# Gate and up products of both FFNs by a seven-product scheme (Strassen–Winograd), with FFN features in three phases

## The chip, the cores and the metric

The kernel runs on one core of a Trainium2 chip. The metric is the device time of one execution in microseconds; lower is better. The time before is the median of three runs, 1134.87 us (1134.28 to 1135.37). The engines are called as in the profile: PE (matmuls; PEld loads its stationary tiles), DVE and POOL (elementwise), ACT (copies and activations), SP (issues the transfers; it computes nothing).

## What is computed

One decoder block on x of 512 tokens by 1024 features, in f32: a SwiGLU FFN, a token mixer (latent attention beside a short convolution) and a second FFN. Each has a norm that is scaled and shifted by vectors that come from a condition c through `w_ada`, and a gated residual. Cut to what matters here:

```
mod = (silu(c) @ w_ada + b_ada).reshape(b, 3, 3, 1024)          # 72 columns of 128 features
h = rms_norm(x, norm_w[0]) * (1 + mod[:, 0, 1]) + mod[:, 0, 0]
g, u = split(h @ w13[0])                                        # w13: 1024 x 5632
x = x + 0.5 * mod[:, 0, 2] * ((silu(g) * u) @ w2[0])            # w2: 2816 x 1024
x = x + mod[:, 1, 2] * mixer(modulated norm of x)
x = x + 0.5 * mod[:, 2, 2] * swiglu(modulated norm of x, w13[1], w2[1])
```

## The kernel before

**Products.** Features lie on the partitions, tokens on the free axis. The 1024 features of h are 8 chunks of 128; the 2816 features of an FFN are 22 groups of 128, each with a gate and an up part (a pair). Every f32 operand is split into hi + lo, both in a reduced f32 form (fp32r): hi by a copy on ACT (L78), lo by a subtraction on DVE (L79). One 128x128 tile of weights against tokens is then three matmuls, hi·hi, hi·lo and lo·hi (`mm3`, L98 to L101), each over 512 tokens, or over 256 where half of the tokens is taken. Weights come as 512 KB loads (`wr`), and are split one unit of work ahead of their products (`stream`, L314).

**An FFN.** The first pairs (`FIRST`: three in FFN1, two in FFN2) are taken chunk by chunk as the norm delivers h: tiles `pf` of PSUM against weights `wf` that stay in 8 KiB blocks (L412 to L449). FFN1 takes them over 512 tokens at the start of the program, where the norm waits for the first vectors of `mod`; FFN2 takes them in two halves of the tokens, under the second half of the mixer's output and its norm. The other 19 and 20 pairs go through `whole` (L322): the gate over 8 chunks into `p_g`, then the up part into `p_u`, 48 matmuls of 512 columns in a pair; `evac` takes silu of the gate on ACT (`sg`), the product with up on DVE (`av`, L401) and its split into `a`.

**Down products.** `out_rows` (L336) makes the 8 output chunks, `w` in the profile, each over all 22 feature groups, with weights in groups of 8, 8 and 6. The last three chunks of FFN1 and the last one of FFN2 are taken in two halves of 256 tokens, so that the norm of the first half lies under the products of the second. A chunk ends with the residual on DVE (L308) and a store to DRAM.

**Condition vectors.** The shift and scale of the first norm come at the start. The other seven vectors are 56 units of work (`ada_unit`, L206), each 0.5 MB of weights and two multiply-adds of 128x512 on DVE (L159); every eighth ends with transposes on PE and a reduction. FFN1 takes three units with each of its 19 full pairs until all are done (L228), with loads of 1 MB.

**Order.** A scheduler fixes each engine's order from the order of the code and from the pools of buffers: 13 blocks of 8 KiB, 11 and 4 slots of 2 KiB, four loads and four hi and lo tiles of weights, three PSUM banks for long products and five for short ones. Loads are issued by SP in program order as their buffers come free.

The full pairs and the first pairs in the code:

```
units.append(whole(f"g{i}_{f}", (w13a, w13b)[i][f - first, 0], KD, norm.h, gate_done))
units.append(whole(f"u{i}_{f}", (w13a, w13b)[i][f - first, 1], KD, norm.h, up_done))
units += out_rows(f"w2{i}", lambda m: w2[i, m], [(0, 8), (8, 8), (16, 6)], a_pieces, res, next_norm, pace)
...
for t in range(nt):
    mm3(ps[t][:, c0:c1], cols(wf[k], t * P, P), cols(norm.h[k], c0, c1 - c0), k == 0, k == KD - 1)
```

## Time and profile before

| | |
|---|---|
| time, median of three runs | 1134.87 us |
| span of the profiled execution | 1133.9 us |
| last startup chunk split, first full pair of FFN1 | 73.09 us, 78.56 us |
| first down product of FFN1, end of FFN1 | 296.93 us, 421.33 us |
| first full pair of FFN2 | 783.79 us |
| end | 1133.9 us |

The profile is one execution. Its span runs from the first instruction to the last, in microseconds from its start; it lies 1.0 us under the median of the three runs and 0.4 us under the fastest of them (1134.28), so times of the trace and times of runs can be set against each other directly. Groups of instructions are rows "line engine operation out<-in shapes xcount | busy us, mean ns of one | idle time before them". A matmul's end is modelled in this trace, and its row is longer than the time until the next one starts; what a matmul costs in a stream is read from the starts in the timeline.

### The profile page before, as it was taken

Reading aid. Unit: us, or ns where it says so; the run is one execution under the profiler, and the core shown is the slowest. Engines: PE = TensorE matmul, PEld = TensorE weight load, DVE = VectorE, ACT = ScalarE, POOL = GpSimd, SP = SyncE. Lnnn points to the kernel's source line nnn. Section 1 sums busy time; section 2 is a strip of 40 time slices with the busy share of each in tenths; the row PEclk is TensorE's granted clock in tenths of the full one; section 3 lists DMA queues with packets and bytes.
Section 4 is the critical chain, followed back from the end, with each engine's and each line's share of the span. In section 5 each row is a group of like instructions: output and inputs, shape, how many; then the busy total and the mean of one; then the engine's idle time right before and its main releaser. Section 6 shows DMA issues by size and latency. Waiting matters only on the chain.

```text
span 1133.9 us, 14667 instructions
## 1 busy us (share of the span) xinstructions
PE 1106.5 (98%) x5574; PEld 918.5 (81%) x5574; DVE 621.8 (55%) x1143; ACT 410.8 (36%) x774; POOL 68.4 (6%) x76
## 2 busy tenths in 40 slices
PE   4799999999999999999999999999999999999998
PEld 3688788788788998888888778899888888888888
DVE  6976767776533586777556554474333333332233
ACT  4343323333222464544434433353333333322222
POOL 4620000000000003110100000000000000000000
PEclk9889999999999999999999999999999999999999
DMA  8645566655444563221323344671222222224432
GB/s 344 223 149 204 188 241 248 248 189 206 158 137 133 178 204 118 58 83 42 89 98 98 113 139 132 204 231 38 94 93 93 93 93 93 93 84 139 123 119 71
DMA packets 50487, 161.04 MB, mean 142 GB/s; under 512 B 5744, under 2 KB 9712, under 8 KB 45808
## 3 DMA queue, kind: packets, MB, share of 16 engines
q1 hardware_dynamic: 50416, 160.10, 42.1%
q8 instruction: 44, 0.72, 0.3%
q14 instruction: 27, 0.22, 0.1%
HBM read 150.64 MB, written 9.44 MB: 141 GB/s over the span
## 4 chain that ended last, share of the span: by engine, by line
PE 91%; DVE 5%; DMA 2%; issue 1%; ACT 1%; POOL 0%; SPq 0%; DVEq 0%; ACTq 0%
PE w L99 7%; PE w L100 7%; PE w L101 7%; PE p_u L101 6%; PE p_g L99 6%; PE p_g L100 6%; PE p_u L99 6%; PE p_u L100 6%; PE p_g L101 6%; PE p_gate L99 3%; PE p_gate L100 2%; PE p_gate L101 2%; PE pf L99 2%; PE pf L100 1%; PE pf L101 1%; PE p_br L99 1%
## 5 line engine op out<-in xcount | busy, mean ns | idle before, releaser
L79 DVE TENSOR_TENSOR wl_w<-wr_w,wh_w 128x512 fp32r<-128x512 f32 x120 | 77.4, 646 | 142.1 <-ACT wh_w L78 139.3
L99 PE MATMUL w<-a,wh_w 128*128 128x512 f32 (+1 forms) x440 | 153.2, 348 | 0.0
L100 PE MATMUL w<-a,wh_w 128*128 128x512 f32 (+1 forms) x440 | 153.0, 348 | 0.0
L101 PE MATMUL w<-a,wl_w 128*128 128x512 f32 (+1 forms) x440 | 152.9, 348 | 0.0
L78 ACT CAST wh_w<-wr_w 128x512 fp32r<-128x512 f32 x120 | 70.1, 584 | 172.0 <-PE w L100 150.3
L99 PE MATMUL p_g<-hh,wh_g 128*128 128x512 f32 x312 | 123.4, 396 | 0.0
L100 PE MATMUL p_g<-hl,wh_g 128*128 128x512 f32 x312 | 123.4, 396 | 0.0
L101 PE MATMUL p_u<-hh,wl_u 128*128 128x512 f32 x312 | 123.4, 396 | 0.0
L99 PE MATMUL p_u<-hh,wh_u 128*128 128x512 f32 x312 | 123.4, 396 | 0.0
L101 PE MATMUL p_g<-hh,wl_g 128*128 128x512 f32 x312 | 123.4, 396 | 0.0
L100 PE MATMUL p_u<-hl,wh_u 128*128 128x512 f32 x312 | 123.2, 395 | 0.0
L78 ACT CAST wh_u<-wr_u 128x512 fp32r<-128x512 f32 x78 | 48.4, 621 | 143.1 <-PE p_u L100 82.4
L79 DVE TENSOR_TENSOR wl_g<-wr_g,wh_g 128x512 fp32r<-128x512 f32 x78 | 55.1, 707 | 73.8 <-ACT wh_g L78 73.3
L78 ACT CAST wh_g<-wr_g 128x512 fp32r<-128x512 f32 x78 | 48.4, 622 | 129.2 <-PE p_g L100 127.3
L99 PEld LDWEIGHTS w<-a,wh_w 128*128 128x128 f32 x440 | 82.6, 188 | 12.2
L100 PEld LDWEIGHTS w<-a,wh_w 128*128 128x128 f32 x440 | 82.6, 188 | 12.1
L101 PEld LDWEIGHTS w<-a,wl_w 128*128 128x128 f32 x440 | 82.6, 188 | 11.9
L79 DVE TENSOR_TENSOR wl_u<-wr_u,wh_u 128x512 fp32r<-128x512 f32 x78 | 53.4, 689 | 56.2 <-ACT wh_u L78 56.2
L99 PEld LDWEIGHTS p_u<-hh,wh_u 128*128 128x128 f32 x312 | 58.6, 188 | 14.2
L101 PEld LDWEIGHTS p_u<-hh,wl_u 128*128 128x128 f32 x312 | 58.6, 188 | 14.2
L100 PEld LDWEIGHTS p_u<-hl,wh_u 128*128 128x128 f32 x312 | 58.6, 188 | 14.1
L101 PEld LDWEIGHTS p_g<-hh,wl_g 128*128 128x128 f32 x312 | 58.6, 188 | 14.1
(299 smaller groups left out, 2116.0 us busy)
## 6 DMA issues: line engine op xcount, KB each, us to landing
ada<-in_ada_dram SPq DMA_DIRECT2D x36, 1024.0 KB, 8.6
wr_w<-in_w_dram SPq DMA_DIRECT2D x40, 512.0 KB, 3.5
wr_g<-in_w13b_dram SPq DMA_DIRECT2D x20, 512.0 KB, 3.5
wr_u<-in_w13b_dram SPq DMA_DIRECT2D x20, 512.0 KB, 3.5
wr_g<-in_w13a_dram SPq DMA_DIRECT2D x19, 512.0 KB, 3.7
wr_u<-in_w13a_dram SPq DMA_DIRECT2D x19, 512.0 KB, 4.2
wr_gate<-in_w_cg_dram SPq DMA_DIRECT2D x16, 512.0 KB, 3.7
wr_w<-in_w_dram SPq DMA_DIRECT2D x20, 384.0 KB, 3.3
```

Source lines behind the costliest of these rows:

```text
L78: nc.scalar.copy(out=hi, in_=src)
L79: nc.vector.tensor_tensor(out=lo, in0=src, in1=hi.bitcast(F32), op=ALU.subtract)
L99: nc.tensor.matmul(ps, a[0], b[0], start=first, stop=False)
L100: nc.tensor.matmul(ps, a[0], b[1], start=False, stop=False)
L101: nc.tensor.matmul(ps, a[1], b[0], start=False, stop=last)
```

## The change

**Seven products.** A full pair is a 2 by 2 block product: weights in two halves of the contraction (4 chunks each), of gate (G1, G2) and up (U1, U2); h in two halves of the contraction and two halves of the tokens (B11, B12, B21, B22). In place of the eight block products stand seven, each 4 chunks by 3 matmuls of 256 columns, 84 matmuls in a pair (`PRODUCTS`, `pair_job`). They need four sums of weights, Z1 = U1 + U2, Z3 = U1 + G1, Z2 = Z1 + G1 and Z4 = Z2 + G2, and four sums of tokens (t1 to T4). Five 256 KB blocks are loaded plainly by SP (two of them the same block); two DMAs issued by GpSimd then add g1 and u2 onto blocks in SBUF, which gives Z3 and Z1; DVE adds the other two. The splits are three of 128x1024 and one of 128x512 a pair (`split_wide`). The token sums are made once in an FFN (`Norm.sums`: four subtractions or additions of 128x256 on DVE and a split of 128x1024, for each of four chunk pairs). The results are combined on ACT (`s`) and DVE (`y`, `u`, and `g` in its bank).

**Phases.** The features go in three phases (`PHASES`): the pairs of a phase, then its share of all 8 output chunks (`down_job`, all matmuls over 256 columns). The partial sums of the first two phases are stored to DRAM (`yd`), loaded again and added on DVE. Only the last phase has the residual.

**The rest.** `FIRST` is two pairs in both FFNs, and FFN1's are taken in matmuls of 256 columns; `Norm.chunk` makes the shifted x in place, with one more operation on ACT; the weights of FFN2's first pairs have their buffers after the mixer's pool is closed (`enter`), and POOL no longer splits a part of FFN1's. Of the 56 units of condition vectors, 24 stand in the first two down phases of FFN1, in loads of 0.5 MB, and 32 in the mixer's `whole` (`ada_step(1)`).

```
-FIRST = (3, 2)
+FIRST = (2, 2)
+PHASES = (((0, 6), (6, 14), (14, 22)), ((0, 8), (8, 16), (16, 22)))
+PRODUCTS = (("Z3", "T3", 1, 0), ("G1", "B11", 0, 0), ("U2", "T4", 1, 1), ("Z1", "t1", 0, 1),
+            ("Z2", "T2", 1, 0), ("G2", "B21", 0, 0), ("Z4", "B22", 0, 1))
...
+        def sums(self, i):
+            (b11, b12), (b21, b22) = ((x[:, :HALF], x[:, HALF:]) for x in (self.x[i], self.x[i + 4]))
+            t = wide(f"T{self.sub}_{i}")
+            t1, t3, t2, t4 = (t[:, q * HALF : (q + 1) * HALF] for q in range(4))
+            for o, p, q, op in ((t1, b11, b12, ALU.subtract), (t3, b12, b22, ALU.subtract), (t2, t1, b22, ALU.add),
+                                (t4, b21, t2, ALU.subtract)):
+                nc.vector.tensor_tensor(out=o, in0=p, in1=q, op=op)
+            b = block(f"T{self.sub}_{i}", F32R)
+            split_to(b[:, :WMAX], b[:, WMAX:], t)
...
     def whole(name, src, n, rhs, done):
...
                     if k == n - 1:
                         done(ps)
+                        ada_step(1)
...
+        def pair_job(f):
+            def prep(w):
+                sa, sb = block(f"sa{name}"), block(f"sb{name}")
+                g1, g2, u1, u2 = (src[r][:, z * T : (z + 1) * T] for r in range(2) for z in range(2))
+                for s, q, part in ((sa, 0, u1), (sa, 3, u1), (sa, 1, g1), (sa, 2, u2), (sb, 1, g2)):
+                    nc.sync.dma_start(out=s[:, q * T : (q + 1) * T], in_=part)
+                nc.gpsimd.dma_start(out=sa[:, :T], in_=g1, accum_op=ALU.add)
+                nc.gpsimd.dma_start(out=sa[:, 3 * T :], in_=u2, accum_op=ALU.add)
+                a, b = (s.rearrange("p (q n) -> p q n", n=T) for s in (sa, sb))
+                split_wide(w, sa[:, : 2 * T], ("Z3", "G1"), f"w0_{name}")
+                yield
+                nc.vector.tensor_tensor(out=b[:, 0], in0=a[:, 3], in1=a[:, 1], op=ALU.add)
+                split_wide(w, sa[:, 2 * T :], ("U2", "Z1"), f"w1_{name}")
+                yield
+                nc.vector.tensor_tensor(out=b[:, 3], in0=b[:, 0], in1=b[:, 1], op=ALU.add)
+                split_wide(w, sb[:, : 2 * T], ("Z2", "G2"), f"w2_{name}")
+                yield
+                split_wide(w, sb[:, 3 * T :], ("Z4",), f"w3_{name}")
+            def body(w):
+                banks = mm(f"g{name}"), aux(f"u{name}")
...
+                product(0)
+                s = short("sum", 3 * HALF, f"s{name}")
+                nc.scalar.copy(out=s[:, T:], in_=halves[1][0])
+                product(1)
+                yield
+                product(2)
+                product(3)
+                nc.scalar.copy(out=s[:, :T], in_=gate)
+                yield
+                product(4)
...
+                nc.vector.tensor_tensor(out=y, in0=halves[1][0], in1=s[:, :HALF], op=ALU.subtract)
+                nc.vector.tensor_tensor(out=u[:, HALF:].rearrange("p (q n) -> p q n", n=HALF),
+                                        in0=y.unsqueeze(1).to_broadcast([P, 2, HALF]),
+                                        in1=s[:, HALF:].rearrange("p (q n) -> p q n", n=HALF), op=ALU.subtract)
+                nc.vector.tensor_tensor(out=u[:, :HALF], in0=halves[1][1], in1=y, op=ALU.add)
+                product(5)
+                yield
+                product(6)
+                nc.vector.tensor_tensor(out=halves[0][1], in0=halves[0][1], in1=u[:, T:], op=ALU.subtract)
+                evac(f, gate, u[:, :T])
...
+        def down_job(phase, m, c0, c1, n_last):
...
+                for k in range(n):
+                    for h0 in range(c0, c1, HALF):
+                        mm3(ps[:, h0 : h0 + HALF], cols(wt, k * P, P), cols(a_pieces[f0 + k], h0, HALF),
+                            k == 0 and h0 == c0, k == n - 1 and h0 == c1 - HALF)
+                if not final:
+                    y = part[m] if phase else slot(f"y{name}")
+                    if phase:
+                        nc.vector.tensor_tensor(out=y, in0=ps, in1=y, op=ALU.add)
+                    else:
+                        nc.scalar.copy(out=y, in_=ps)
+                    nc.sync.dma_start(out=yd[phase % 2][m], in_=y)
+                    if i == 0:
+                        ada_step(2 if m % 2 == phase % 2 else 1)
```

**Where the instructions move.** First, DVE at the end of FFN1's first pairs. `av_*` and `a_*` are the activations, `wl_g_4` is the lo part of the second full pair's gate weights, `T_*` are the token sums, `sb_2` and `w_0_2_l` the weight sum and lo part of the first full pair (pair 2); each row is the line, the operation, out<-in and the shape. Before:

```order
L401 TENSOR_TENSOR av_0_633<-sg_0_631,pf_1_182 128x512
L401 TENSOR_TENSOR av_1_639<-sg_1_637,pf_3_184 128x512
L79 TENSOR_TENSOR a_0_630<-av_0_633,a_0_630 128x512
L401 TENSOR_TENSOR av_2_646<-sg_2_644,pf_5_186 128x512
L79 TENSOR_TENSOR a_0_630<-av_1_639,a_0_630 128x512
```

And now (where lines are left out before the last two rows, the rope tables stand, L679 to L699):

```order
L338 TENSOR_TENSOR T_3_660<-x_in_74,x_in_75 128x256
L338 TENSOR_TENSOR T_3_660<-T_3_660,x_in_75 128x256
L501 TENSOR_TENSOR av_0_669<-av_0_669,pf_1_182 128x512
L109 TENSOR_TENSOR T_2_657<-T_2_652,T_2_657 128x1024
L338 TENSOR_TENSOR T_3_660<-x_in_75,T_3_660 128x256
L501 TENSOR_TENSOR av_1_674<-av_1_674,pf_3_184 128x512
...
L109 TENSOR_TENSOR T_3_665<-T_3_660,T_3_665 128x1024
L109 TENSOR_TENSOR a_0_668<-av_0_669,a_0_668 128x512
L109 TENSOR_TENSOR a_0_668<-av_1_674,a_0_668 128x512
...
L534 TENSOR_TENSOR sb_2_718<-sa_2_717 128x512
L109 TENSOR_TENSOR w_0_2_l<-sa_2_717,w_0_2_h 128x1024 x2
```

The weights of the first full pair were split ahead of the first pairs' activations; now they are split behind all token sums, activations and rope tables.

Second, SP in FFN1's down products. `wr_w` and `wr_d` are down weights, `ada` and `wr_ada` the condition's weights, `yd` stores of partial sums. Before:

```order
L83 DMA wr_w_0_2_2463<-in_w_dram 128x768
L209 DMA ada_4_2323<-in_ada_dram 128x2048
L209 DMA ada_6_2407<-in_ada_dram 128x2048
L83 DMA wr_w_0_0_2499<-in_w_dram 128x1024
L83 DMA wr_w_0_1_2533<-in_w_dram 128x1024
L83 DMA wr_w_0_2_2568<-in_w_dram 128x768
```

Now, in the first phase:

```order
L113 DMA wr_d_0_5_0_1463<-in_w_dram 128x768
L113 DMA wr_ada_6_1484<-in_ada_dram 128x1024
L625 DMA yd_0_179<-yd_0_4_0_1481 128x512
L113 DMA wr_ada_7_1488<-in_ada_dram 128x1024
L113 DMA wr_d_0_6_0_1532<-in_w_dram 128x768
L625 DMA yd_0_179<-yd_0_5_0_1550 128x512
L113 DMA wr_ada_0_1553<-in_ada_dram 128x1024
L113 DMA wr_d_0_7_0_1583<-in_w_dram 128x768
```

Down weights, condition weights and stores of partial sums now alternate, where the condition weights had nearly all come beside the pairs.

Third, DVE in a full pair of FFN1. Before (pair 7 being prepared, pair 6 being finished):

```order
L159 SCALAR_TENSOR_TENSOR ada_acc_1_961<-ada_0_958,c_act,ada_acc_1_961 128x512
L79 TENSOR_TENSOR wl_g_7_512_1006<-wr_g_7_999,wh_g_7_512_1005 128x512
L79 TENSOR_TENSOR wl_u_7_0_1052<-wr_u_7_1049,wh_u_7_0_1051 128x512
L401 TENSOR_TENSOR av_6_1037<-sg_6_1035,p_u_6_1009 128x512
L79 TENSOR_TENSOR wl_u_7_512_1056<-wr_u_7_1049,wh_u_7_512_1055 128x512
L79 TENSOR_TENSOR a_6_1034<-av_6_1037,a_6_1034 128x512
```

Now (pair 13 being prepared, pairs 11 and 12 being finished):

```order
L109 TENSOR_TENSOR w_0_13_l<-sa_13_2469,w_0_13_h 128x1024
L501 TENSOR_TENSOR av_11_2433<-av_11_2433,u_11_2398 128x512
L534 TENSOR_TENSOR sb_13_2470<-sa_13_2469 128x512
L109 TENSOR_TENSOR a_10_2306<-av_11_2433,a_10_2306 128x512
L564 TENSOR_TENSOR y_12_2525<-u_12_2442,s_12_2455 128x256
L537 TENSOR_TENSOR sb_13_2470<-sb_13_2470 128x512
L565 TENSOR_TENSOR u_12_2524<-y_12_2525,s_12_2455 128x512
L568 TENSOR_TENSOR u_12_2524<-u_12_2442,y_12_2525 128x256
L109 TENSOR_TENSOR w_0_13_l<-sb_13_2470,w_0_13_h 128x1024
L572 TENSOR_TENSOR g_12_2441<-g_12_2441,u_12_2524 128x256
L109 TENSOR_TENSOR w_0_13_hl<-sb_13_2470,w_0_13_hl 128x512
L501 TENSOR_TENSOR av_12_2560<-av_12_2560,u_12_2524 128x512
```

The condition's multiply-adds are gone from the pairs, and the combination of the seven products stands among the splits of the next pair's weights; `y` needs the fifth product of the pair in work, and what stands behind it in the row waits with it.

More of the change, by code (lines that the diff above doesn't have):

```diff
@@ L230, in ada_step, with chunks, __init__, x @@
             ada_unit(*ada_todo.pop(0))
+    def chunks(tiles):
+        return [tiles[k // 4][:, (k % 4) * T : (k % 4 + 1) * T] for k in range(KD)]
     class Norm:
-        def __init__(self, sub, x):
-            self.sub, self.x, self.acc, self.last, self.steps = sub, x, None, {}, iter(())
-            self.h = []
+        def __init__(self, sub, tiles):
+            self.sub, self.acc, self.steps = sub, None, iter(())
+            self.tiles = tiles
+            self.h, self.pairs, self.tsums = [], [], []
+        @property
+        def x(self):
+            return chunks(self.tiles)
         def add(self, k, c0=0, n=T):
@@ L285, in prepare, with operand @@
+        def operand(self, name, i):
+            which, q = OPERANDS[name]
+            b = (self.pairs, self.tsums)[which][i]
+            return tuple(b[:, z * WMAX + q * HALF : z * WMAX + (q + 1) * HALF] for z in range(2))
         def prepare(self, b0, nb):
@@ L455, in ffn @@
             rope_tables()
-        drain(rest)
+        run(jobs)
     rope_tab = {}
@@ L517, in tile_hybrid_block @@
     r1 = Residual(1, xT, 2, x1d)
-    n1 = Norm(1, r1.x)
-    ffn(0, n0, ((0, T),), first_chunk, 3, r1, n1, (0, 1, 1, 2, 2, 2, 1, 0, 0))
+    n1 = Norm(1, r1.tiles)
+    ffn(0, n0, ((0, T),), first_chunk, r1, n1, (0, 2, 3, 3))
+    next(n1.steps)
+    enter("mixer")
     wc = []
@@ L795, in tile_hybrid_block @@
     drain(latent_products(0))
-    next(n1.steps)
     second = latent_products(1)
```

233 lines of the change are left out of this document (166 added, 67 removed).

## The prediction

> **What bounds the kernel now.** I read the page's first part and the chain of waits first, then windows by stage, then the groups by form, then the starts in the timeline.
>
> ```profile
> span 1133.9 us, 14667 instructions
> PE 1106.5 (98%) x5574; PEld 918.5 (81%) x5574; DVE 621.8 (55%) x1143; ACT 410.8 (36%) x774; POOL 68.4 (6%) x76
> PE 91%; DVE 5%; DMA 2%; issue 1%; ACT 1%; POOL 0%; SPq 0%; DVEq 0%; ACTq 0%
> ```
>
> PE is the bound nearly everywhere: 98% busy and 91% of the chain. So matmul time that goes is worth its full price, unless another engine or the DMAs take its place. The windows show who is near to that (columns: PE, PEld, DVE, ACT and POOL busy, granted clock, DMA share, GB/s):
>
> ```profile
> 80.00:200.00 120.00, 120.00 (x528) 96.60 (x527) 84.67 (x154) 38.37 (x66) 2.81 (x8) 1.00 0.59 224
> 380.00:410.00 30.00, 30.00 (x265) 29.95 (x263) 19.38 (x37) 15.85 (x30) 0.84 (x1) 1.00 0.67 200
> 410.00:500.00 90.00, 88.60 (x572) 79.97 (x571) 70.34 (x164) 50.31 (x123) 14.82 (x11) 1.00 0.35 110
> 740.00:775.00 35.00, 34.14 (x283) 33.84 (x282) 28.82 (x62) 18.08 (x36) 2.16 (x2) 1.00 0.62 196
> 900.00:1000.00 100.00, 100.00 (x430) 80.60 (x429) 35.87 (x53) 32.49 (x54) 0.00 (x0) 1.00 0.28 90
> ```
>
> In FFN1's pairs DVE is 71% busy and the DMAs 59%; in FFN2's pairs 36% and 28%. Both have room there, little at the start of the mixer (DVE 78%) and before FFN2 (82%). GB/s over share gives what the DMA engines move at full use: 380 in 80:200, 321 in 900:1000, 299 in 380:410.
>
> The groups give counts; a matmul's end is modelled, so its price is read from starts.
>
> ```profile
> L99 PE MATMUL p_g<-hh,wh_g 128*128 128x512 f32 x312 | 123.4, 396 | 0.0
> L99 PE MATMUL w<-a,wh_w 128*128 128x512 f32 x264 | 104.2, 395 | 0.0
> L99 PE MATMUL w<-a,wh_w 128*128 128x256 f32 x176 | 48.9, 278 | 0.0
> ```
>
> ```profile
> 24.02 2.50 PE L99 MATMUL pf<-hh,wfh 128*128 128x512 f32 x5
> ...
> 29.39 0.51 PE L101 MATMUL pf<-hh,wfl 128*128 128x512 f32 x1
> ...
> 78.56 0.40 PE L99 MATMUL p_g<-hh,wh_g 128*128 128x512 f32 x1
> ...
> 199.61 0.39 PE L99 MATMUL p_u<-hh,wh_u 128*128 128x512 f32 x1
> ...
> 204.28 0.39 PE L101 MATMUL p_u<-hh,wl_u 128*128 128x512 f32 x1
> ...
> 296.93 0.39 PE L99 MATMUL w<-a,wh_w 128*128 128x512 f32 x1
> ...
> 763.82 0.28 PE L101 MATMUL pf<-hh,wfl 128*128 128x256 f32 x1
> ...
> 765.98 0.28 PE L101 MATMUL pf<-hh,wfl 128*128 128x256 f32 x1
> ...
> 783.79 0.40 PE L99 MATMUL p_g<-hh,wh_g 128*128 128x512 f32 x1
> ...
> 1117.76 0.28 PE L100 MATMUL w<-a,wh_w 128*128 128x256 f32 x1
> ...
> 1130.45 0.28 PE L101 MATMUL w<-a,wl_w 128*128 128x256 f32 x1
> ```
>
> From 199.61 to 204.28 are 20 steps, 233.5 ns; over longer stretches I read 233.3. From 1117.76 to 1130.45 are 112 steps of 256 columns, 113.3 ns; from 763.82 to 765.98 are 18, 120.0 ns. So half the columns cost a little under half in one place and a little over half in the other. From 24.02 to 29.39, after PE had idled, 13 steps of 512 columns take 413 ns each: the clock is granted low for a while.
>
> **The change, part by part.**
>
> *Pairs.* Each matmul group of `p_g` and `p_u` has 312: 6 x 312 / 48 = 39 pairs, 39 x 48 x 233.3 ns = 436.8 us. Now 40 pairs of 84 matmuls. The two rows bound their price: 113.3 where the stationary tile lies in the streamed pool (`wh_w`), 120.0 where it lies in a long-lived block (`wfh`). The new weights are streamed tiles, so I take 115: 40 x 84 x 115 = 386.4 us, a gain of 50.4 (17.6 less at 120.2, 5.7 more at 113.3). The seven-for-eight saving needs 84 matmuls of 256 to beat 48 of 512, that is, under 133.3 ns each; both rows are under it.
>
> The Trainium skill, page "TensorE: Matmul & The Clock Gate", section "Back-to-back issue gap", gives sustained streams with weight loads 81 ns at 128 columns and 131 at 512; a straight line between them, an estimate, is 98 ns at 256, and by it a pair would grow from 6.3 to 8.2 us. The trace contradicts it: 512 columns take 233.3 ns here, not 131.
>
> *Down products.* 3 x 264 of 512 and 3 x 176 of 256 columns: 184.8 + 59.8 = 244.6 us. Now 2112 of 256 at 113.3: 239.3, a gain of 5.3 (14.6 less at 120.2).
>
> *FFN1's start.*
>
> ```profile
> 70.03 0.69 DVE L79 TENSOR_TENSOR wl_u<-wr_u,wh_u 128x512 fp32r<-128x512 f32 x1
> 70.63 0.22 DVE L147 TENSOR_TENSOR mod<-ps,pk 128x1 f32<-128x1 f32 x2
> ...
> 73.09 0.75 DVE L283 SCALAR_TENSOR_TENSOR hl<-ht,mod,hh 128x512 fp32r<-128x512 f32 x1 [0.79 <-ACT hh L282]
> ...
> 760.03 0.48 DVE L308 SCALAR_TENSOR_TENSOR x<-wo,mod,xin 128x256 f32<-128x256 f32 x1
> 760.42 0.48 DVE L283 SCALAR_TENSOR_TENSOR hl<-ht,mod,hh 128x256 fp32r<-128x256 f32 x1
> ```
>
> ```profile
> L79 DVE TENSOR_TENSOR wl_w<-wr_w,wh_w 128x512 fp32r<-128x512 f32 x100 | 69.0, 690 | 117.2 <-ACT wh_w L78 114.4 <-PE w L100 2.7
> L159 DVE SCALAR_TENSOR_TENSOR ada_acc<-ada,c_act,ada_acc 128x512 f32<-128x512 f32 x98 | 68.0, 746 | 0.0
> L79 DVE TENSOR_TENSOR wl_w<-wr_w,wh_w 128x256 fp32r<-128x256 f32 x20 | 8.5, 425 | 24.8 <-ACT wh_w L78 24.8
> L79 DVE TENSOR_TENSOR wo<-wr_wo,wo 128x1024 fp32r<-128x1024 f32 x3 | 3.7, 1219 | 0.1
> ```
>
> Back to back, a 512 split takes 0.60 us from start to start (70.03 to 70.63), 0.09 under its 690 ns; so I count 0.34 for 256 columns, 1.13 for 1024, and 0.40 for a 256 step with a scalar (760.03 to 760.42). The last chunk's split ends at 73.84. Now four 512 splits fewer stand ahead of it (-2.4), three token sums more (+1.0), and one ACT step more lies in its chain (+0.7): 73.1. By DVE's order there follow 10 of the sums (3.4), the four 1024 splits of them (4.5), two `av` and two `a` (2.4), the rope tables (20 small steps, 2.2 by the 0.22 us for two at 70.63), a weight sum (0.6) and the first lo part (1.1): 14.2, so the third matmul of the first full pair waits until about 87 (84 to 91; POOL gives up its share of the startup and 1 MB less is loaded, which may bring it forward). In place of 78.56: +8.4. The former cover, a third pair in `pf`, is gone. PE idles some 12 us and then runs at the low clock: +2.3, as the 13 steps of 413 ns lost 0.18 us each.
>
> *FFN2's start.* After the last output chunk is taken at 760.03, DVE now still has: rest of the first half's chunks (2.8), eight 512 splits of `wf` (4.8), the norm and the second half's chunks (6.5), 16 sums and four splits (10.0), `av` and `a` (2.4), a weight sum and the first lo (1.7): 28.2, and some 3 of waits for loads whose buffers come late: 792 in place of 783.79, +8.2 (4 to 13), and +2 at the low clock.
>
> *Pairs on DVE.* By durations a pair asks three 1219, one 690 (splits), two 690 (weight sums), 425 + 690 + 425 + 425 (combination), two 690 (`av`, `a`): 9.1 us; back to back 8.0. A pair on PE takes 9.66, or 9.81 with the stalls below. DVE's work fits by 0.6 to 1.7 us, but in a fixed order: `y` waits for the fifth product, 6.9 us into the pair, and a sum and splits of the next pair stand behind it. Following the rows by hand, every second pair's last lo part comes 0.3 to 0.7 us late: I take +6 over 40 pairs (0 to 12).
>
> *The adding DMAs* have no like in this trace. Bound below: nothing. They wait for plain loads of the same block, and splits wait for them; but blocks are loaded a pair ahead, 9.7 us.
>
> ```profile
> wr_w<-in_w_dram SPq DMA_DIRECT2D x40, 512.0 KB, 3.5
> wr_br<-in_w_br_dram SPq DMA_DIRECT2D x16, 256.0 KB, 2.6
> x1d<-x SPq DMA_DIRECT2D x5, 256.0 KB, 2.1
> ```
>
> A plain load of 256 KB lands in 2.6 us; above: at 3.7 times that the add would use up the pair's lead. I take nothing, nearest to the plain row. The Trainium skill, page "DMA: Bandwidth & Descriptors", section "Anatomy of one DMA — SWDGE (gpsimd) path", gives 2.0 us + bytes / 436e3 for GpSimd's DMAs, 2.6 us for this size as an estimate: by it the term would be nothing too; no run here shows it yet. The pairs' demand, seven blocks of 0.26 MB in 9.7 us, is 190 GB/s, under any rate above.
>
> *FFN1's first two down phases.* PE: 8 x 36 and 8 x 48 matmuls, 32.6 and 43.5 us. DMA in them: down weights 2.8 and 4.2 MB, condition weights 6.3 and 6.3, the next two pairs 3.7 and 3.7, partial sums 2.1 and 4.2: 14.9 and 18.4 MB. At 350 GB/s (between 321 and 380) 42.6 and 52.6 us, 19 more than PE; some 7 us of it is loaded early. I take +12 (2 to 34: at 380 with all pair loads early, at 299 with none). FFN2's phases carry no condition weights: they fit.
>
> *Condition vectors.* FFN1 loses 32 units and four rounds of transposes: of the 5.5 us that 78.56 + 19 x 11.2 leaves until 296.93, 3.1 go to the mixer. There 64 steps of 512 (0.66 each) are 42 us more for DVE, over 340 us where it has room outside 410:500; PE pays the 3.1, I add 2 for DVE and 2 for the exchange of pools: FFN1 -3.1, mixer +7 (3 to 17).
>
> *Sum:* -50.4 - 5.3 - 3.1 + 8.4 + 2.3 + 8.2 + 2 + 6 + 12 + 7 = -12.9, from 1133.9 to 1121.0; runs lie 1.0 above the profiled span: **1122**.
>
> **The rivals.**
>
> *All is covered:* matmuls at 113.3, no pair stalls, no phase stalls: 5.7 + 6 + 12 = 23.7 less, 1098. For: DVE and DMA averages fit. Against: the order of `y`.
>
> *The pair is paced by DVE* (slower side): by durations it has 9.1 of 9.66 us, and each split waits for its ACT copy first. It decides from a pair of 9.81 + 12.9 / 40 = 10.1 us on; at 10.6 it costs 32: 1154. For: six kinds of hand-over between ACT, PE and DVE in a pair, in one fixed order. Against: back to back it is 8.0.
>
> *DMA paces the first two phases* at 299 GB/s, as 380:410 moved with stores among the loads: 34 in place of 12, 1144.
>
> *256 columns cost 120.2*, as in `pf`: 17.5 + 14.6 more, 1154. Against: `w`, the nearest like, is at 113.3.
>
> *A matmul has a high fixed price*, so that half the columns cost three quarters (175 ns by 233.3): 84 x 175 is 3.5 us a pair more than now, +140. The Trainium skill's section on the back-to-back gap, cited above, would have it so. The rows at 113.3 and 120.0 all but exclude it.
>
> *The saving isn't there* because PE is busy by name only: excluded by steady starts at 233.3.
>
> **How the numbers follow.** Forecast 60%, of which 4% lie within 0.2% (2.3 us, about what a measurement can tell from no change); all covered 14%; DVE-paced pairs 10%; DMA-paced phases 8%; 120.2 ns 6%; the last two together 2%. Faster: 56 + 14 = 70%; slower: 10 + 8 + 6 + 2 = 26%. The range, 1098 to 1150, takes in the forecast with its bounds, half of the covered case and the DMA-paced one.
>
> **What would show it.** Pairs: starts 113 to 116 ns apart, 9.7 to 10.1 us a pair; over 10.1 DVE or a DMA ends PE's waits, and the row before the late split says which. FFN1's first full pair at 84 to 91 behind an idle PE that waits for `w_0_2_l`; FFN2's at 788 to 797 less what came earlier. In phases 0 and 1 of FFN1 a DMA share near 1 with PE waiting for `d_0` or `d_1` splits. If PE's idle time sums to much over 50 us, I am wrong on the costs; if its busy time hardly falls, on the gain.

## The result, and the profile after

The changed kernel takes 1225.78 us (median of four runs, 1225.02 to 1230.59); the kernel before took 1135.12 beside it. The ratio is 1.081, 95% interval 1.0795 to 1.0824: slower by 91 us, where 1122 was forecast and at most 1150 was in the range. The profiled execution has a span of 1223.7 us.

The changed kernel's page, its first part, its transfers, and the chain that ended last:

```profile
span 1223.7 us, 20051 instructions
PE 1090.4 (89%) x7886; PEld 1014.9 (83%) x7886; DVE 809.3 (66%) x1393; ACT 497.8 (41%) x835; POOL 133.3 (11%) x149
q1 hardware_dynamic: 79648, 181.61, 45.2%
q0 software_dynamic: 11520, 20.98, 9.9%
PE 61%; DMA 16%; DVE 13%; issue 4%; ACT 3%; POOL 2%; SPq 1%; DVEq 0%; POOLq 0%; ACTq 0%
```

PE has 61% of the chain in place of 91%: DMA has 16% in place of 2%, DVE 13% in place of 5%. No engine is full. So this isn't an engine that became the bound; it is waits. Where they lie shows in the starts of the first and last products of each stage (the row's last bracket is the wait ahead of it):

```profile
84.44 0.28 PE L132 MATMUL pf<-h,wfl 128*128 128x256 f32 x1
...
96.31 0.58 PE L130 MATMUL u<-T,w_h 128*128 128x256 f32 x1 [11.60 <-ACT w_h L108]
...
146.79 0.28 PE L130 MATMUL d<-a,d_h 128*128 128x256 f32 x1
...
206.01 0.28 PE L130 MATMUL u<-T,w_h 128*128 128x256 f32 x1
...
285.97 0.28 PE L130 MATMUL d<-a,d_h 128*128 128x256 f32 x1
...
353.66 0.28 PE L132 MATMUL g<-h,w_l 128*128 128x256 f32 x1
...
436.01 0.28 PE L130 MATMUL d<-a,d_h 128*128 128x256 f32 x1
...
490.76 0.72 PE L130 MATMUL pc<-wc,h 128*128 128x416 f32 x1 [4.10 <-ACT wc L108]
...
861.56 0.58 PE L130 MATMUL pf<-h,wfh 128*128 128x256 f32 x1 [4.91 <-ACT wfh L108]
...
891.04 0.39 PE L130 MATMUL u<-T,w_h 128*128 128x256 f32 x1 [2.65 <-ACT w_h L108]
```

Stage by stage, from these rows and their like in both traces (the mixer runs from the start of FFN1's last product to that of the last `wo` product, 421.2 to 759.3 us before and 483.8 to 856.4 now):

| stage | before | after | difference | forecast, stalls of it included |
|---|---|---|---|---|
| until FFN1's first full pair | 78.6 | 96.3 | +17.8 | +10.7 |
| FFN1's full pairs (19 before, 20 now) | 218.4 | 212.8 | -5.6 | -19 |
| FFN1's down products | 124.3 | 174.7 | +50.4 | +10 |
| mixer | 338.1 | 372.6 | +34.5 | +7 |
| FFN2 until its first full pair | 24.5 | 34.7 | +10.2 | +10.2 |
| FFN2's full pairs | 224.0 | 195.2 | -28.8 | -28 |
| FFN2's down products to the end | 126.1 | 137.5 | +11.4 | -3 |

The saving is there where it was looked for, in FFN2's pairs. The stages that lost add up to 124 us, of which FFN1's down products have 50, the mixer 34, FFN1's start 18, and FFN2's start and down products 10 and 11; the pairs gave back 34. The waits of PE in FFN1's first two down phases, first 146:210 and behind the gap 286:350 (engine, what waits <- for what: us in total, times, longest):

```profile
PE d L130 <- ACT d_h L108: 7.4, 3, 4.5
PE d L130 <- ACT a L108: 2.7, 1, 2.7
PE d L132 <- DVE d_l L109: 2.6, 4, 1.4
...
PE d L132 <- DVE d_l L109: 5.3, 3, 3.7
PE d L130 <- ACT d_h L108: 3.8, 3, 3.0
PE d L130 <- ACT a L108: 3.7, 1, 3.7
```

And those of SP's queue in 146:210:

```profile
SPq L625 <- ACT yd L624: 45.4, 8, 9.5
```

PE waits for the hi and lo parts of down weights (`d_h`, `d_l`). SP stands for 45.4 of 64 us at the stores of partial sums (L625), each of which waits for ACT's copy (`yd`), and so for the end of a chunk's products. What stands behind in SP's row waits too, as some of its starts show:

```profile
155.92 0.33 SPq L625 DMA_DIRECT2D yd<-yd  x1
156.30 0.42 SPq L528 DMA_DIRECT2D sb<-in_w13a_dram  x1
156.82 0.41 SPq L113 DMA_DIRECT2D wr_ada<-in_ada_dram  x1
162.03 0.33 SPq L625 DMA_DIRECT2D yd<-yd  x1
162.45 0.38 SPq L113 DMA_DIRECT2D wr_d<-in_w_dram  x1
166.24 0.33 SPq L625 DMA_DIRECT2D yd<-yd  x1
```

And by stretches (columns as in the prediction): those two phases, and for comparison a stretch of FFN1's pairs:

```profile
147.00:206.00 59.00, 43.94 (x296) 41.47 (x295) 23.91 (x36) 12.01 (x17) 1.73 (x2) 0.86 0.65 203
286.00:354.00 68.00, 52.85 (x400) 50.57 (x398) 31.96 (x45) 9.47 (x11) 1.72 (x2) 0.92 0.74 225
...
220.00:280.00 60.00, 59.70 (x515) 59.30 (x514) 49.17 (x72) 33.41 (x49) 6.93 (x8) 1.00 0.59 149
```

The DMA engines are busy 65% and 74%, not full, and the granted clock (third column from the right) falls to 0.86 and 0.92: behind waits PE runs at half clock for a while. Over the whole execution the low clock was granted for 114 us, 14 before.

### The profile page after: what moved, and what is told of

Read it like the earlier page. It is cut to its first block, busy times and chain, and to the rows that moved or that the text cites. A ratio compares the mean times of both kernels' runs of the same rounds, so it can differ in the third digit from the quotient of the medians.

```text
span 1223.7 us, 20051 instructions
## 1 busy us (share of the span) xinstructions
PE 1090.4 (89%) x7886; PEld 1014.9 (83%) x7886; DVE 809.3 (66%) x1393; ACT 497.8 (41%) x835; POOL 133.3 (11%) x149
## 3 DMA queue, kind: packets, MB, share of 16 engines
q1 hardware_dynamic: 79648, 181.61, 45.2%
## 4 chain that ended last, share of the span: by engine, by line
PE 61%; DMA 16%; DVE 13%; issue 4%; ACT 3%; POOL 2%; SPq 1%; DVEq 0%; POOLq 0%; ACTq 0%
DMA sa<-in_w13a_dram 5%; DMA wr_ada<-in_ada_dram 5%; PE d L132 4%; PE d L131 4%; PE d L130 4%; PE g L132 4%; PE g L130 4%; PE g L131 4%; PE u L132 4%; PE u L131 4%; PE u L130 4%; DMA wr_d<-in_w_dram 2%; DMA sa<-in_w13b_dram 2%; PE p_gate L132 2%; PE p_gate L130 2%
## 5 line engine op out<-in xcount | busy, mean ns | idle before, releaser
L130 PE MATMUL d<-a,d_h 128*128 128x256 f32 x628 | 182.0, 290 | 22.2 <-ACT d_h L108 11.7
L132 PE MATMUL d<-a,d_l 128*128 128x256 f32 x628 | 181.4, 289 | 9.8 <-DVE d_l L109 9.7
L131 PE MATMUL d<-a,d_h 128*128 128x256 f32 x628 | 180.5, 287 | 1.0 <-DVE a L109 0.7
L130 PE MATMUL u<-T,w_h 128*128 128x256 f32 x480 | 134.3, 280 | 14.3 <-ACT w_h L108 14.2
L130 PEld LDWEIGHTS d<-a,d_h 128*128 128x128 f32 x628 | 124.7, 199 | 24.6 <-ACT d_h L108 13.3
L132 PE MATMUL u<-T,w_l 128*128 128x256 f32 x480 | 135.2, 282 | 3.8 <-DVE w_l L109 3.5
L132 PEld LDWEIGHTS d<-a,d_l 128*128 128x128 f32 x628 | 124.4, 198 | 12.0 <-DVE d_l L109 11.9
L131 PE MATMUL u<-T,w_h 128*128 128x256 f32 x480 | 133.9, 279 | 0.0
L131 PEld LDWEIGHTS d<-a,d_h 128*128 128x128 f32 x628 | 124.8, 199 | 2.0 <-DVE a L109 2.0
L109 DVE TENSOR_TENSOR w_l<-sa,w_h 128x1024 fp32r<-128x1024 f32 x80 | 96.7, 1224 | 12.1 <-PE d L131 4.2
L130 PEld LDWEIGHTS u<-T,w_h 128*128 128x128 f32 x480 | 91.3, 190 | 14.9 <-ACT w_h L108 14.7
L132 PEld LDWEIGHTS u<-T,w_l 128*128 128x128 f32 x480 | 91.2, 190 | 6.3 <-DVE w_l L109 6.3
L130 PE MATMUL g<-h,w_h 128*128 128x256 f32 x320 | 90.2, 282 | 6.9 <-ACT s L559 6.5
L131 PEld LDWEIGHTS u<-T,w_h 128*128 128x128 f32 x480 | 91.1, 190 | 0.0
L131 PE MATMUL g<-h,w_h 128*128 128x256 f32 x320 | 89.9, 281 | 0.0
```

Of the source, the lines that this page charges most:

```text
L109: nc.vector.tensor_tensor(out=lo, in0=src, in1=hi.bitcast(F32), op=ALU.subtract)
L130: nc.tensor.matmul(ps, a[0], b[0], start=first, stop=False, skip_group_check=parts)
L131: nc.tensor.matmul(ps, a[0], b[1], start=False, stop=False, skip_group_check=parts)
L132: nc.tensor.matmul(ps, a[1], b[0], start=False, stop=last, skip_group_check=parts)
```

## The experiments

Two theories stood against each other for the phases: Q, that the loads come late because they stand in SP's row behind stores that wait for results, and its rival, that there are too many bytes for the time. For the start, theory O is that the order of POOL's and DVE's work (the rope tables ahead of the first pairs) delays the adding DMAs; for the mixer, theory W is that DVE waits there for the condition weights' loads. Stage lengths below are from the starts of PE's rows, as in the table; the mixer stage is here taken from the first `pc` product to the first `pf` product of FFN2 (370.8 us in the changed kernel). A time without an interval is one run, and a stage length is read from one trace: four runs of the kernel with the orders together lay between 1187.5 and 1199.5, and mixer stages of kernels that leave the mixer alone between 368.6 and 373.5, so differences of this size between single runs say nothing. One fact has to stand ahead of the others: the step of a matmul, the time from its start to the next one's, depends on where its weights lie in SBUF (below, "the address"). The kernels here keep the addresses of the changed kernel, unless said.

**Stores of partial sums on ACT.**

```
-nc.sync.dma_start(out=yd[phase % 2][m], in_=y)
+nc.scalar.dma_start(out=yd[phase % 2][m], in_=y)
```

> The stores of partial sums are issued by ACT in place of SP; nothing else is changed. Theory Q (SP's order: the next chunk's down weights are issued only behind the store of a chunk that PE has yet to finish): FFN1's first two down phases, 59 and 62 us in the changed kernel, come to 36 to 46 and 46 to 53; FFN2's, 45 and 50, to 44 to 46 each; time about 1190. Rival B (bytes: the transfers of the phases take longer than their products): FFN1's phases stay at 55 or more each, time over 1215.

1205.5 us. The two phases took 54.1 and 59.0 us (59.2 and 67.7 in the changed kernel; the 62 of the expectation leaves out the end of the second), FFN2's 44.7 and 49.7. SP's order costs something, about 14 us of these phases, but theory Q foresaw 36 to 46 in the first, and the time lies between the two theories. With the stores gone, SP waits mostly for buffers that PE's products still read:

```profile
SPq L113 <- PE d L132: 16.2, 4, 5.6
SPq L113 <- DMA yd<-yd: 8.1, 4, 4.7
SPq L113 <- PE d L131: 5.2, 1, 5.2
```

**Without condition vectors.** `ada_todo = []`, and constants in `mod` for the seven vectors.

> All 56 units of the condition vectors are left out (their loads, multiply-adds, transposes); the seven vectors are constants. Theory B (bytes): FFN1's first two down phases fall to 33 to 36 and 44 to 46 us. Theory Q (SP's order): the stores still stand ahead of the down weights, which only land sooner: 42 to 54 and 48 to 56. For the mixer, 366 us from its first to its last product against 338 before: if the units there cost it, 338 to 345; if it lost for another reason (the exchange of pools, the split form), 355 or more. Time 1140 to 1165 if the units explain both, over 1190 if neither.

1170.6 us. The mixer fell from 372.6 to 340.8 by the stages of the table, so the units cost it there. But FFN2's pairs, which the edit doesn't touch, had become slower, 205 us in place of 195. The starts in the pairs show why:

```profile
230.00 0.28 PE L132 MATMUL g<-h,w_l 128*128 128x256 f32 x1
230.12 0.28 PE L130 MATMUL g<-h,w_h 128*128 128x256 f32 x1
230.24 0.28 PE L131 MATMUL g<-h,w_h 128*128 128x256 f32 x1
230.36 0.28 PE L132 MATMUL g<-h,w_l 128*128 128x256 f32 x1
```

120 ns everywhere, where the changed kernel has 113 to 118. The edit had also dropped two tiles of 32 bytes that stood ahead of the weight buffers, which so moved by 64 bytes. So its stages don't compare with the changed kernel's. The same kernel, with the addresses kept:

> As the kernel without condition vectors (all 56 units left out, constants in their place), but two small tiles are kept so that the streamed weights lie at the addresses of the changed kernel, 64 bytes off a multiple of 128; in the run before this one they had slid to a multiple of 128, and every matmul of 256 columns there took 120 ns, every one of 512 took 226.5. Theory A (the address of the stationary tile sets the step): 113.3 and 233.3 ns again, about 1142. Rival (the step came from something else in that run): 120 and 226.5 again, about 1170. With 113.3, FFN1's first two down phases at 33 to 38 and 44 to 48 us would lay their loss on the units wholly.

1158.7 us, with 113 to 118 ns in place of 120, and 233 for 512 columns. The address does set the step, but not to the last ns: the median was 117 here and 113 in the changed kernel, FFN2's pairs took 200.6 us, and the time missed 1142; what makes 117 of 113 stays open. FFN1's first two down phases took 35.9 and 49.8 us, the mixer stage 343.7 in place of 370.8. So the 56 units cost 23 + 18 us in the phases and 27 in the mixer, 68 together. Not all of it is the price of their new places: the kernel before has these units too, and pays at least for their transposes (5.5 us by the prediction's reading); it wasn't run without them.

**Loads or multiply-adds.** Two halves of that: the units' loads alone (`raw_load` stays, `scale_add` and the rest go), and their arithmetic alone, on a tile that is on chip.

> The 56 units' loads stay, their multiply-adds, transposes and reductions are left out (constants in place of the vectors), addresses as in the changed kernel. If the loads cost it (bytes, or the buffers and SP's places they take): FFN1's first two down phases stay at 52 or more and 58 or more us. If DVE's waits for these loads cost it (lo parts of the down weights stand behind a multiply-add that waits): 34 to 44 and 45 to 52. The mixer: 340 to 350 if the multiply-adds cost it there, 358 or more if the loads' turns in its four buffers do. Time 1150 to 1165 if DVE, over 1180 if the loads.

> The other half: the 56 units' multiply-adds, transposes and reductions stay but read a tile that is on chip, their loads are left out (the seven vectors are not the reference's). If the loads cost it: FFN1's first two down phases at 33 to 40 and 44 to 50 us, and the mixer at 340 to 350. If DVE's work itself costs it: the phases at 45 or more and 55 or more, the mixer at 358 or more. Time 1145 to 1165 if the loads or the waits for them, over 1190 if the work.

1189.2 and 1166.4 us.

| | first phase | second phase | mixer stage |
|---|---|---|---|
| changed kernel | 59.2 | 67.7 | 370.8 |
| loads only | 52.4 | 70.1 | 344.6 |
| arithmetic only | 34.1 | 52.0 | 355.2 |
| neither | 35.9 | 49.8 | 343.7 |

In the phases it is the loads: by themselves they cost 16.5 of the 23.3 us in the first and all of it in the second, the arithmetic by itself some 2 at most. In the mixer it is the arithmetic (11.5 us by itself, of which 3.3 are the steps of its transposes on PE), and with the loads as well 27; the loads alone cost 1.

**Half the bytes.** `raw_load(ada[v - 2, k // 2][:, k % 2, :T], T, ...)`, each unit using its half twice.

> Each of the 56 units loads half of its columns and uses them twice (so the seven vectors are not the reference's): the same count of loads, multiply-adds and buffers, half the bytes. If bytes cost it in FFN1's first two down phases (59 and 68 us from the first down product to the next pair, 36 and 50 without units): 47 to 50 and 57 to 60. If the places in SP's order and in the ten buffers cost it, whatever their size: 55 to 59 and 63 to 68.

1204.3 us; the phases at 48.5 and 55.6. Halving the bytes gives back 10.7 of 23.3 and 12.1 of 17.9 us, 46% and 68%. So the rival of bytes has the larger part of what the units cost in the phases. Even so the DMA engines weren't full (0.65 to 0.74 busy in the changed kernel). The reading that fits both, which no run shows by itself: loads stand one behind the other, each issued when a buffer or a store lets it, and each holds up the next for as long as its bytes take. The stores' place in SP's row is a part of that chain (14 us).

**Eight plain products in the same structure.** No sums of weights or tokens, no adding DMAs, no combination; all else as changed.

```
+PRODUCTS = (("G1", "B11", 0, 0), ("G1", "B12", 0, 1), ("U1", "B11", 1, 0), ("U1", "B12", 1, 1),
+            ("G2", "B21", 0, 0), ("G2", "B22", 0, 1), ("U2", "B21", 1, 0), ("U2", "B22", 1, 1))
...
+for s, q, part in ((sa, 0, g1), (sa, 1, u1), (sa, 2, g2), (sa, 3, u2)):
+    nc.sync.dma_start(out=s[:, q * T : (q + 1) * T], in_=part)
```

> The changed kernel with eight plain block products of 256 columns in a pair (96 matmuls), no sums of weights or tokens, no adding DMAs, no combination; phases, units, order and buffers as changed. By the starts alone a pair takes 10.9 us in place of 9.5, +54 us over 40 pairs. If the seven products do bring their matmuls' time: pairs of FFN2 11.0 each (9.8 in the changed kernel), and FFN1's first full pair, without sums of tokens, at 84 to 90 in place of 96.3; the phases as before within 5 us; time 1250 to 1275. If the sums and the combination eat it: pairs no more than 0.5 us longer, time under 1235.

1207.7 us: faster than the changed kernel by 18, against both expectations. FFN2's pairs took 10.9 us as the count of matmuls says (87.0 for eight, 77.2 with seven products), so the seven products do bring their time: 25 us in FFN2 and 14 in FFN1's pairs. But FFN1's first full pair started at 84.8 in place of 96.3, its first two down phases took 41.5 and 50.8 in place of 59.2 and 67.7, and FFN2's second 43.5 in place of 50.3. The page has what is gone from the transfers:

```profile
span 1205.9 us, 20054 instructions
PE 1119.2 (93%) x8366; PEld 1050.4 (87%) x8366; DVE 606.3 (50%) x1033; ACT 391.3 (32%) x667; POOL 63.3 (5%) x69
q1 hardware_dynamic: 73888, 171.12, 42.6%
```

No adding DMAs (21.0 MB), and 10.5 MB less in plain loads. So 11.5 + 34.6 us of loss in FFN1, and 10.2 in FFN2's down products, belong to the seven products and no other part of the change. What of the seven products it is, no run takes apart. One part is bytes, seven blocks for a pair in place of four: the two phases of FFN1 moved 9.1 and 13.0 MB here (223 GB/s in 41 us, 255 in 51) where the changed kernel moved 12.0 and 15.3. Another stands in the changed kernel's trace, in DVE's row. Its waits for the adding DMAs of the next phase's pairs, in 146:210 and in 286:350, and two such places with what stood behind them:

```profile
DVE sb L534 <- DMA sa<-in_w13a_dram: 7.7, 2, 4.4
...
DVE sb L534 <- DMA sa<-in_w13a_dram: 14.8, 2, 9.9
```

```profile
308.24 0.69 DVE L534 TENSOR_TENSOR sb<-sa 128x512 f32<-128x512 f32 x1 [9.92 <-DMA sa<-in_w13a_dram]
308.85 0.69 DVE L622 TENSOR_TENSOR yd<-d,yd 128x512 f32<-128x512 f32 x1
309.56 0.33 SPq L625 DMA_DIRECT2D yd<-yd  x1
...
1080.00 0.69 DVE L534 TENSOR_TENSOR sb<-sa 128x512 f32<-128x512 f32 x1 [5.72 <-DMA sa<-in_w13b_dram]
1080.61 0.68 DVE L501 TENSOR_TENSOR av<-av,u 128x512 f32<-128x512 f32 x1
```

The weight sum `sb` of the next phase's pair stands in DVE's fixed order ahead of work that PE and SP need now: the sum of partial results `yd` (SP stood 10.4 us at its store), lo parts of down weights, and the last pair's activation `av`. In FFN2's second phase that makes nearly all of the 6.8 us: PE waits 3.4 us for `a`, with half the clock granted from 1081 to 1088. With eight products these waits of DVE are gone, and its waits for condition weights are not (16.8 us in the first phase of either kernel).

**Rope tables later.** `rope_tables()` behind the third full pair (`if i == 0 and f == 4`) in place of ahead of the first.

> The rope tables are made behind the third full pair of FFN1 in place of ahead of the first; nothing else is changed. Theory O (in-order ACT and POOL: the first pair's hi copy stands behind the rope's sine on ACT, the second pair's adding DMAs stand behind the rope's products on POOL): first full pair at 92 to 94 in place of 96.3, the stall of 6.7 us at 105.9 gone, the low clock behind it shorter; time 10 to 16 less, about 1212. Rival (the second pair's adds are late because its blocks come free late, or because an adding DMA itself is slow): the stall of 6 us stays, time 2 to 4 less.

1211.1 us. The first full pair starts at 91.6; the stage of FFN1's first four pairs 41.7 in place of 50.5, its stall of 6.5 us gone. Theory O holds. In the changed kernel POOL's row shows it:

```profile
95.06 1.04 POOL L708 TENSOR_TENSOR rt_qsin<-pk,rope_tmp 128x64 f32<-128x64 f32 x2 [23.30 <-ACT rope_tmp L701]
...
99.14 2.03 POOL L708 TENSOR_TENSOR rt_kcos<-pk,rope_tmp 128x64 f32<-128x64 f32 x2
101.11 0.87 POOL L529 DMA_DIRECT2D sa<-in_w13a_dram  x1
```

The adding DMAs of the second full pair are instructions of POOL and stood behind six us of rope products (95.06 to 101.11), which stood behind ACT's sine, which stood behind DVE's rope steps.

**The mixer's condition weights in blocks,** in 1 MB loads as in the kernel before, issued by SP, and then by GpSimd:

```
+both = block(f"ada_{v}_{k}")
+nc.sync.dma_start(out=both.rearrange("p (u c) -> p u c", u=2), in_=ada[v - 2, k // 2])
```

> In the mixer the condition weights come as 1 MB loads into 8 KiB blocks, as in the kernel before, in place of the four buffers that the mixer's own weights use; nothing else is changed. Theory W (the loads take turns with the mixer's weights in four buffers, come late, and DVE's multiply-adds stand waiting for them with the attention's steps behind): the mixer, 366 us, comes to 340 to 352, DVE's wait for these loads from some 22 us there to under 6; time about 1205. Rival D (the 64 multiply-adds, 42 us, are simply too much for DVE there): 360 or more, time over 1218.

> In the mixer the condition weights come in 1 MB loads into 8 KiB blocks, issued by GpSimd in place of SP; nothing else is changed. If what stays of the mixer's loss lies in SP's order (its weights' loads behind loads that wait for a block): the mixer, 367 us with the same loads on SP, comes to 352 to 358, time 1208 to 1214. If the transfers' presence beside DVE's work costs it otherwise: 363 or more, time over 1219.

1225.7 and 1220.8 us; the mixer stage 366.6 and 364.5 (370.8). DVE's waits for these loads in the mixer fell from 21.9 us to 4.0 and 5.2, and only 4 to 6 us came back, little more than single traces differ by: theory W falls, and SP's order isn't it either. The arithmetic's 11.5 us stand; why loads beside it add some 10 to 15 more stays open. In the changed kernel PE's waits there are mostly for late steps of the attention (`pTl` 7.0 us and `kTl` 4.6, both from DVE).

**Units back in FFN1's pairs,** three to each, none elsewhere.

> One part of the change undone: the condition vectors' units stand three to a full pair of FFN1, as in the kernel before, and in none of its down phases nor in the mixer. FFN1's first two down phases come to about 36 and 50 us and the mixer to about 344, as without units: 69 us less. DVE then has 8.0 to 9.1 us and 3 x 1.3 in each of 19 pairs, 12 to 13.1 us, so FFN1's pairs, 213 us together, come to 245 to 265. Time 1188 to 1208. If DVE's waits for these loads add to its work, the pairs take over 270 and the time is over 1212.

1281.9 us. The phases fell to 42 and 54 and the mixer stage to 343, but the pairs took 319 us: 15.9 each, more than DVE's work asks. In 203:329 DVE is busy 70% and PE 75%:

```profile
203.00:329.00 126.00, 93.88 (x699) 89.27 (x697) 87.68 (x135) 42.33 (x60) 12.20 (x14) 0.85 0.64 196
```

The units share ten 4 KiB buffers with the pairs' hi and lo parts, and loads of pairs stand behind units in SP's row; from 96 to 330 us DVE stood 37.9 us at the same sum `sb`, whose block came late. None of the places tried is free for the units in this layout; FFN2's first pairs, for the vector that is needed last, weren't tried.

**Orders together.** First three: stores on ACT, rope late, and the start's condition loads ahead of the first pairs' weights; then the first two alone; then these two with the mixer's blocks by GpSimd.

> The changed kernel with three changes of order and none of work: stores of partial sums issued by ACT, rope tables behind the third full pair, and at the start each chunk's condition load issued ahead of the first pairs' weights. If the gains of the first two add up (20.3 and 14.6 against 1225.8) and the third brings FFN1's first full pair forward by 2 to 5 us: 1185 to 1190. Rival (the stalls take each other's place): over 1195.

> Stores of partial sums on ACT and rope tables behind the third full pair, without the third change of order, which put FFN1's first full pair back from 91.6 to 96.3. If the two add up: 1189 to 1193, first full pair at 91.6. Rival: near 1200, as with three.

> The orders that helped together: stores on ACT, rope tables late, the mixer's condition weights in blocks issued by GpSimd. If all add up: 1176 to 1186 where the mixer gains, 1189 to 1195 where it doesn't. By either it stays slower than the kernel before, 1134.

1200.8 (1.0584 of before, 1.0566 to 1.0601), 1195.7, and 1193.3 (1.0526, 1.0477 to 1.0575). The third order was a mistake: the first full pair went back to 96.3, where it is 90.6 with two. Orders give back 30 to 33 of the 91 us, a little less than the sum of the first two alone (35).

**The address.** In all kernels but the last of these, moving operands lie at a multiple of 128 bytes in a partition; the streamed weights lie 64 bytes off it in the kernel before and in the changed one, those in long-lived blocks on it. Three kernels make a table of it: the one without condition vectors, and two forms of the kernel before, of which the first drops a tile of 64 bytes (`cs = mod_col(v, 0, KD)`), and the second adds 64 bytes at the start of SBUF as well. These two distances, 0 and 64, are all that occur.

> The kernel before, with one change: the sums of the condition vectors go straight to their columns, so a tile of 64 bytes is gone and the streamed weights' buffers move by 64 bytes to a multiple of 128, where the moving operands lie. Theory A: 3600 matmuls of 512 columns take 226.5 in place of 233.3 ns (-24.5 us), 528 of 256 take 120 in place of 113.3 (+3.5): about 1113. Rival: no change, 1134.

> The kernel before without the small tile, and with 64 bytes more at the start of SBUF: now moving and streamed stationary operands both lie 64 bytes off a multiple of 128. If the stationary tile's own address sets the step: 233.3 and 113.3 ns, about 1134. If its place relative to the moving operand does: 226.5 and 120, about 1115.

1115.75 us (ratio to before 0.9827, 0.981 to 0.9844), and 1116.4. Its starts, 512 columns and 256:

```profile
229.82 0.39 PE L99 MATMUL p_u<-hh,wh_u 128*128 128x512 f32 x1
230.05 0.39 PE L100 MATMUL p_u<-hl,wh_u 128*128 128x512 f32 x1
230.28 0.39 PE L101 MATMUL p_u<-hh,wl_u 128*128 128x512 f32 x1
...
1099.78 0.28 PE L100 MATMUL w<-a,wh_w 128*128 128x256 f32 x1
1099.90 0.28 PE L101 MATMUL w<-a,wl_w 128*128 128x256 f32 x1
1100.02 0.28 PE L99 MATMUL w<-a,wh_w 128*128 128x256 f32 x1
```

| weights against moving operand, modulo 128 bytes | 512 columns | 256 columns |
|---|---|---|
| equal (both 0, or both 64) | 226.5 | 120 |
| 64 apart | 233.3 | 113.3 (up to 118) |

It is the place of one relative to the other that counts. This kernel, the one before with 64 bytes moved, beats both: 19 us under before, 110 under the changed one. It also moves the price of the seven products: 48 x 226.5 is 10.9 us, against 84 x 113.3 = 9.5, a saving of 1.35 us a pair and not 1.7. FFN2, where the change came out 7 us ahead of before, would come out about even with this one, which takes 366.0 us from its last `wo` product to the end, the changed kernel 367.3; this last is worked out from two traces, not run as one kernel.

## Why the prediction was wrong, point by point

Of the signs that the prediction named, the one for wrong costs came: PE's idle time is 133 us (27 before). FFN1's first full pair started at 96.3, not at 84 to 91, and waited first for the hi part `w_h` from ACT. PE waited for the splits of `d_0` and `d_1` as named, but at a DMA share of 0.65 and 0.74, not near 1.

**The pairs' matmuls: right.** 115 ns was taken, the changed kernel has 113 to 118. That the nearest row was the right one is partly luck: the prediction put 113.3 and 120.0 down to the pool, and it is the address. FFN2's pairs took 9.76 us each, 9.81 was forecast with stalls. The rival of DVE-paced pairs didn't come: DVE's order costs little where nothing else is in its way. But that is FFN2; FFN1's pairs cost 10.6 each, and two thirds of that excess lie in the first four (50.5 us), most of it by POOL's queue (41.7 with the rope later).

**The rule of the back-to-back gap** (the Trainium skill, "TensorE: Matmul & The Clock Gate", section "Back-to-back issue gap") gave 131 ns for 512 columns; the traces give 226.5 or 233.3. What split these two is the address, which the section doesn't have.

**FFN1's down phases: the step that failed most.** "I take +12 (2 to 34)" was +51: 59.2 and 67.7 us, for 32.6 and 43.5 of products. The bytes were counted a little high (14.9 and 18.4 MB, some of it loaded early; the two stretches moved 12.0 and 15.3), and 2.8 MB of down weights are 3.1; nor does the lower bound come out of its own terms, which give 0. None of this made the miss. Two steps were wrong. First, the sum divided bytes by the rate at full use, 350 GB/s, as if loads could always run. They didn't: the DMA engines moved 203 and 225 GB/s at 65 and 74%, while SP stood 45.4 of 64 us at stores. The order in the document showed the stores between the loads of SP; I read it as bytes and not as waits. The units' loads are the larger part of it (41 us go without the units, 23 with half of their bytes). Second, the next pairs' blocks stood in that sum as plain bytes, and the wait for their adding DMAs at nothing, because "blocks are loaded a pair ahead". At the phase boundaries that lead was gone, and DVE stood at the weight sum with the phase's own work behind it, 7.7 and 14.8 us; without the seven products the phases take 17 us less each. The rival priced at 1144 came nearest, with 34 for 51, but it too had full DMA engines in it.

**FFN1's start.** +10.7 was +17.8. Of DVE's row the work was counted right: from the end of the last chunk's split (79.4) to that of the first lo part (97.7) it took 18.3 us, 14.2 forecast, and 2.5 of the difference are waits for ACT. But the last chunk itself came 5.5 us later than before, not 0.7 earlier, and the rope's way through ACT and POOL was left out: moving the tables, of which 2.2 us stood in the sum as DVE's work, took 4.7 us off ahead of the first pair and 8.7 in the first four. POOL is the queue that the adding DMAs were moved to, and the one whose order I didn't look at.

**The mixer.** +7 was +34. That DVE "has room" there was read from its busy share (78% at the start, then 61, 58 and 48%). The attention there is a chain of DVE, ACT and PE steps; the units' arithmetic, 42 us of it put into DVE's gaps, made the stage 11.5 us longer (3.3 of it the transposes, which the sum had), and 27 with the loads. What makes up the last 15 isn't settled. The exchange of pools between FFN1 and the mixer, 2 in the sum, is 7.0 from the last down product to `pc`, 0.1 before.

**FFN2's start: right in its sum** (+10.2 forecast, +10.2); 4.9 us of it are a wait for `wfh` ahead of the first `pf` product, where the forecast had 3 for such waits. **FFN2's down products** were to gain 3 and lost 11: 10 of it goes without the seven products. In the second phase it isn't their bytes but the wait for the last pair's `a`, held up in DVE's row by the next pair's weight sum as shown above, and the low clock behind it.

**The low clock** was counted twice, at the starts, with 4.3 us. It came with waits all over the execution: 114 us were granted at half clock, so up to 57 us of PE's work were lost to it beside the waits themselves, 7 before.

**The adding DMAs** were taken at nothing. In their queue 21.0 MB took 9.9% of the DMA engines' span, which is 173 GB/s at full use; plain loads and stores moved 181.6 MB in 45.2%, 328 GB/s. The queue by itself doesn't make it: where GpSimd also issued the mixer's blocks, plain loads of 1 MB, the queue moved 16.8 MB more in 45 us more of its time, some 370 GB/s. The adds landed 7.0 us after issue in the median, plain loads of the same blocks 5.7 to 6.3. The Trainium skill's fit ("DMA: Bandwidth & Descriptors", section "Anatomy of one DMA — SWDGE (gpsimd) path") gives an estimate of 2.6 us for this size and says nothing of the add. In pairs that run freely the 7 us were covered, as the forecast had it; at the phase boundaries, where they took up to 10.8 us and were issued late, they weren't.

## What to carry to other kernels

Here PE was busy for 98% of the time because the order kept every buffer and every queue just ahead of it. A change that cuts PE's work by 5% and adds a quarter to the bytes and 30% to DVE's work has to be priced by queues: for each load, what stands ahead of it on its engine, and what that waits for; and for each new wait, what stands behind it on the engine that waits. Put stores that wait for results on another queue than loads that PE needs next; and before comparing two kernels, see that their operands lie alike.

## What the runs showed of the hardware

The step of fp32r matmuls with a weight load each depends on the addresses of weights and moving operand modulo 128 bytes: 226.5 and 120 ns (512 and 256 columns) where they are equal, 233.3 and 113.3 (up to 118) where they are 64 apart; other distances weren't tried. An adding DMA from GpSimd used the DMA engines about 1.9 times as long per byte as the plain transfers of this kernel did (173 against 328 GB/s at full use).
